# Mask added on VectorE in the maximum of the logits, and three rearrangements: first loads, banks of the spatial gate, last token blocks

## The chip, the core and the metric

One core of a Trainium2 chip runs the whole program. Its engines work side by side, each through its own queue in order: TensorE (matrix products into PSUM, weights loaded ahead of each), VectorE and ScalarE (elementwise work, reductions along a row, evacuation of PSUM), GpSimd (here a few powers and masks), and SyncE, whose queue issues most of the DMAs. [...] The metric is the time of one execution in microseconds; less is better.

## The reference

Two layers on 512 tokens of width 1024, fp32, with a memory of 256 rows. Layer 0 mixes by a gated spatial unit over chunks of 128 tokens (6 groups) and by attention to the memory (4 heads of 64); layer 1 by causal attention with a forget gate (12 heads of 64) and again by memory attention. Both are followed by an output projection, a feed-forward of width 2816, and norms. The parts that the change touches:

```python
def block(args):                      # forgetting_attention, one block of 128 queries
    i, qi, ci = args
    qpos = i * Q_BLOCK + jnp.arange(Q_BLOCK)
    logits = jnp.einsum('bthd,bshd->bhts', qi, k).astype(jnp.float32) * scale
    logits = logits + ci[..., :, None] - cT[..., None, :]
    mask = kpos[None, :] <= qpos[:, None]
    logits = jnp.where(mask, logits, -jnp.inf)
    p = jax.nn.softmax(logits, axis=-1).astype(v.dtype)
    return jnp.einsum('bhts,bshd->bthd', p, v)
...
s = jnp.einsum('gts,bcsgd->bctgd', w, vc) + b_s.T[None, None, :, :, None]   # spatial gating
...
f = (jax.nn.silu(f @ w_ffn_gate[layer]) * (f @ w_ffn_up[layer])) @ w_ffn_down[layer]
h = h + rmsnorm(f, ln_ffn_post[layer])                                      # the end of a layer
```

## The kernel before

**Arithmetic and layout.** Activations lie transposed: features on the 128 partitions, 512 tokens along the row, eight tiles for 1024 features. Each fp32 product is three products of rounded parts (`mm3`, L191: hi x hi, hi x lo, lo x hi), accumulated in one PSUM bank. Every weight is loaded as fp32 into one of four `raw` buffers and split into hi (ScalarE, cast) and lo (VectorE, subtract) by `split` (L240). PSUM banks come from three rings: `mm` and `lg` with three banks each, `tr` with two. A tile's bank is free again when its last reader is done, and within a bank the program keeps reads and writes of the same tile apart.

**Order.** A planner puts the instructions of each engine into a queue: by their place in the program, and by when its own costs let them start. `tc.issue_after` (and `behind`, L249) holds an instruction behind another in that order, and `high_priority` moves it forward. On the chip each queue then runs in order and waits by semaphore.

**Start.** `layer_a` (L566) loads the query weights (`query_weights`, two matrices of 512 KB, here half of the first, all of the second, the rest of the first) and the input x (`tokens`, eight tiles of 256 KB, cut in two parts each by `normed_parts`) on SyncE's queue. Sixteen products of three passes (L646) alternate between two outputs, tile by tile, with two dummy products of zeros (`idle`) after the first product of each output. Value and gate products of the gated unit follow as filling between later steps.

**Spatial gate.** `gate_inputs(m)` (L699) makes one block of the gate (24 passes, ring mm). `rows` (L761) are two tiles in ring lg that VectorE folds into the bias `bsp` (L768). `spatial(g)` (L728) makes two PSUM tiles `s`, both in ring lg, each read by ScalarE and VectorE.

**Attention.** `FoxHead.logits(tb)` (L499) makes the logits of 128 queries against the (tb+1) x 128 keys that they may see: one product of the head's parts (L504), one with the rest of the parts and the gate's sums (L505), and one in bf16 that adds the constant `neg` (0 on and below the diagonal, -1e30 above) to the last 128 columns, as identity times `neg` (L506). `weigh` (L437) takes the negated maximum of the row from the bank (VectorE, L440), then exp with that as bias and the row sum as second output (ScalarE, L441) into an SBUF tile p. `norm` divides (L450), `turn` transposes p (TensorE, L457) and splits it, `values` (L517) multiplies with the values. `attend` (L531) staggers this: while one head's logits are made, the head before is transposed and multiplied, and pieces of other work (`between`: key and value products, later the output projection) are laid between in a fixed count per head, five in the first heads, three in the last. There are 12 heads with four blocks of queries each, so 48 mask products.

**End.** `tail_of` (L785) makes, for each block tb of 128 tokens, the last share of the down projection into two banks of 512 columns (ring mm and lg); for the last block the second is cut in two halves of 256 columns (L806), both in the same bank. VectorE adds the earlier share (L816), ScalarE squares and sums (L819), VectorE adds up (L821), GpSimd takes the power (`rsqrt`, r), and ScalarE, in the last block VectorE too, scales by r. `give` (L1359) then transposes the block back (L847), adds it with the gain as per-partition scalar to h, one 128 x 128 piece at a time (`residual`, L852), and sends it out. `give(tb - 1)` stands behind `tail(tb)`; after the last, eight dummy products and `give` of block 3.

Of the kernel before, what the change touches and what calls it, by code (L numbers as in the profile page):

```python
# [7 lines left out]
F32 = mybir.dt.float32  # L8
# [32 lines left out]
def hybrid(ctx: ExitStack, tc: tile.TileContext, i: dict, out: bass.AP):  # L41
# [6 lines left out]
    sp = ctx.enter_context(tc.tile_pool(name="small", bufs=8))  # L48
    pp = ctx.enter_context(tc.tile_pool(name="psum", bufs=3, space=PSUM))
# [69 lines left out]
    G.affine_select(out=neg_f[:, :P], in_=neg_f[:, :P], pattern=[[-1, P]], compare_op=ALU.is_ge,  # L119
                    fill=NEG, base=0, channel_multiplier=1)  # L120
    neg = cp.tile([P, P], BF16, name="neg")
    V.tensor_copy(neg, neg_f[:, :P])
# [307 lines left out]
    class Softmax:  # L430
# [6 lines left out]
        def weigh(self, tb, lg, p):  # L437

            c = slice(tb, tb + 1)
            V.reduce_max(out=self.nmx[:, c], in_=lg, axis=AX.X, negate=True)  # L440
            last_exp[0] = A.activation(p, lg, AF.Exp, bias=self.nmx[:, c], accum_out=self.sm[:, c])  # L441
            self.p[tb] = p
# [47 lines left out]
    class FoxHead(Softmax):  # L490
# [8 lines left out]
        def logits(self, tb):  # L499
            qa, qc, ka, kc = self.parts  # L500
            n = (tb + 1) * P
            c = slice(tb * P, n)
            lg = ps("lg", s="lg")
            PE.matmul(lg[:, :n], qa[:, c], ka[:, :n], start=True, stop=False)  # L504
            PE.matmul(lg[:, :n], qc[:68, c], kc[:68, :n], start=False, stop=False)  # L505
            PE.matmul(lg[:, c], ident_b, neg, start=False, stop=True)  # L506
# [58 lines left out]

    def layer_a():  # L566
# [18 lines left out]
        tokens(0, 1)  # L585
        query_weights(1, 0, 1024)
        tokens(1, 2)
        tokens(2, 4)
# [3 lines left out]
        last_a = tuple(last_parts)  # L592
        vg, evacs = {}, []
# [28 lines left out]
        with tc.tile_pool(name="sgu", bufs=1) as lp:  # L622
# [105 lines left out]
            def spatial(g):  # L728
                t = temp("s", (P, TB, P))
                for tp2 in range(2):  # L730
                    o = ps("lg", (P, 2, 2, P), s="s")
                    hi, lo = vp[g // 2, tp2]
                    c = slice((g % 2) * P, (g % 2 + 1) * P)
                    for n in range(2):
                        PE.matmul(o[:, n, :, :], hi[:, n, c], ws[g], start=True, stop=True)
                        PE.matmul(o[:, n, 0, :], lo[:, n, c], ws[g][:, 0, :], start=False, stop=True, skip_group_check=True)
                    two = t[:, 2 * tp2 : 2 * tp2 + 2, :]
                    A.activation(two, o[:, :, 1, :], AF.Copy, scale=vcols[:, g : g + 1])
                    V.scalar_tensor_tensor(out=two, in0=o[:, :, 0, :], scalar=vcols[:, g : g + 1], in1=two,
                                           op0=ALU.mult, op1=ALU.add)  # L740
# [17 lines left out]
            V.tensor_copy(vcols, o)  # L758

# [25 lines left out]
    def tail_of(xs, load, ys, eps=None, last=False):  # L785
# [12 lines left out]
        def tail(tb, halfway=None):  # L798
# [4 lines left out]
            c = slice(tb, tb + 1)  # L803
            final = last and tb == TB - 1
            two = small("two", 1) if final else None
            at = [(0, 0, 4), (1, 0, 2), (1, 2, 4)] if final else [(0, 0, 4), (1, 0, 4)]  # L806
            for n, (dh, m0, m1) in enumerate(at):
                if m0 == 0:
                    o = ps("lg" if dh else "mm", s="y")
                cols = slice(m0 * P, m1 * P)  # L810
                for k in range(nk):
                    w = [part[:, m0:m1, :] for part in ws[k // 2, dh][k % 2]]
                    end = token_products(o[:, cols], xs[k], w, tb, k == 0, k == nk - 1)
                y = ys[tb][dh][:, cols]
                with urgent(tb):
                    V.tensor_add(y, o[:, cols], y)  # L816
# [3 lines left out]
                    if n == len(at) - 1:  # L820
                        V.scalar_tensor_tensor(out=v[:, c], in0=one, scalar=run, in1=eps[:, c] if eps is not None else rms_eps,  # L821
# [10 lines left out]
            if final:  # L832
                for m in (0, 2):
                    cols = slice(m * P, (m + 2) * P)
                    V.tensor_scalar_mul(ys[tb][1][:, cols], ys[tb][1][:, cols], r[:, c])
                    A.activation(ys[tb][0][:, cols], ys[tb][0][:, cols], AF.Copy, scale=r[:, c])
                return end
            with urgent(tb):
                for y in ys[tb]:
                    A.activation(y, y, AF.Copy, scale=r[:, c])  # L840

        return tail, ys

    def turned(ys, k, tbs, out):

        for n, tb in enumerate(tbs):
            PE.transpose(out[:, n * P : (n + 1) * P], ys[tb][k // 4][:, k % 4 * P : (k % 4 + 1) * P], ident)  # L847
# [510 lines left out]

    def give(tb, order, queues=(nc.sync,)):  # L1359
# [79 lines left out]
```

## Time and profile before

| | |
|---|---|
| median of 3 runs | 1113.27 us (1113.27 to 1113.5) |
| the profiled execution, its time | 1111.68 us |
| its span, first to last instruction | 1110.0 us |
| mean granted TensorE clock | 0.999 |
| opening: first product of the queries to the last one's start | 5.56 to 19.02 us |
| stage of the 12 masked heads | 613 to 718 us |
| from the last product's start to the span's end | 1101.05 to 1110.0 us |

The times of instructions are from the profiled execution. Busy time counts an engine as busy while any of its instructions runs; products on TensorE are pipelined, so their durations overlap, and the chain of work (each step followed back to what released it) tells better how long each one holds the queue. The mean of a group is of one instruction from start to end. In rows of windows stand: the stretch, its length, then busy time and count for TensorE, its weight loads, VectorE, ScalarE and GpSimd, the granted clock, the share of DMA and GB/s. In rows of a timeline: start, length, engine, line, operation, output and inputs, and in brackets the idle time before it and what ended it.

### The profile page before, as it was taken

The numbers are of one execution on the slowest core, as the hardware profiler recorded it, in microseconds if no ns is written. First come the engines' busy times: TensorE is split into PE (matmuls) and PEld (weight loads), VectorE is DVE, ScalarE is ACT, GpSimd is POOL, SyncE is SP. The second block draws the span as 40 slices with busy tenths as digits, with TensorE's granted clock in tenths as the row PEclk, the third lists the DMA queues.
The fourth block names the chain that finished last, engine by engine and source line by source line (L and its number), as shares of the span: only waits on it lengthen the run. The fifth ranks groups of instructions, "written<-read, shape, count | busy, mean of one in ns | idle before, by whom it ended". The sixth has DMA issues, their size and how long they took to land.

```text
span 1110.0 us, 19527 instructions
## 1 busy us (share of the span) xinstructions
PE 1100.9 (99%) x7384; PEld 999.7 (90%) x7385; DVE 895.0 (81%) x1734; ACT 667.1 (60%) x1401; POOL 25.1 (2%) x41
## 2 busy tenths in 40 slices
PE   9999999999999999999999999999999999999998
PEld 6997889999899899998988897889999899899996
DVE  7879659897698598787868889868897698588775
ACT  7776578664366254477647667768665266254453
POOL 0000000000000000001000000000000000000000
PEclk9999999999999999999999999999999999999999
DMA  7521331334135133245222555431234134233222
GB/s 268 159 79 58 113 116 39 115 115 136 55 115 152 56 96 115 79 150 173 77 76 75 155 124 131 129 115 39 77 97 151 58 115 134 58 114 114 77 76 77
DMA packets 63558, 118.13 MB, mean 106 GB/s; under 512 B 5164, under 2 KB 39992, under 8 KB 63464
## 3 DMA queue, kind: packets, MB, share of 16 engines
q1 hardware_dynamic: 62584, 116.05, 34.4%
q8 instruction: 58, 0.95, 0.4%
q0 software_dynamic: 192, 0.52, 0.2%
q10 hardware_dynamic: 688, 0.31, 0.1%
q14 instruction: 36, 0.29, 0.1%
HBM read 104.71 MB, written 2.10 MB: 96 GB/s over the span
## 4 chain that ended last, share of the span: by engine, by line
PE 86%; DVE 3%; ACT 1%; issue 1%; DMA 0%; POOLq 0%; POOL 0%; DVEq 0%; ACTq 0%
PE y L193 10%; PE y L194 10%; PE y L195 10%; PE a L194 5%; PE a L195 5%; PE a L193 5%; PE ps L193 3%; PE ps L194 3%; PE ps L195 3%; PE x L194 3%; PE x L195 3%; PE x L193 3%; PE e L193 3%; PE e L194 3%; PE e L195 3%; PE tr L457 1%
## 5 line engine op out<-in xcount | busy, mean ns | idle before, releaser
L241 ACT CAST whi<-raw 128x512 fp32r<-128x512 f32 x460 | 277.2, 620 | 266.6 <-PE y L195 118.5
L241 DVE TENSOR_TENSOR wlo<-raw,whi 128x512 fp32r<-128x512 f32 x460 | 306.3, 686 | 117.0 <-ACT whi L241 114.6
L193 PE MATMUL y<-whi,fhi 128*128 128x512 f32 (+1 forms) x356 | 139.7, 393 | 0.0
L194 PE MATMUL y<-wlo,fhi 128*128 128x512 f32 (+1 forms) x356 | 139.5, 392 | 0.0
L195 PE MATMUL y<-whi,flo 128*128 128x512 f32 (+1 forms) x356 | 139.1, 391 | 0.0
L194 PE MATMUL x<-xslo,whi 128*128 128x256 f32 x320 | 89.9, 281 | 0.0
L194 PE MATMUL a<-xslo,whi 128*128 128x256 f32 x320 | 89.9, 281 | 0.0
L195 PE MATMUL x<-xshi,wlo 128*128 128x256 f32 x320 | 89.8, 280 | 0.0
L193 PE MATMUL x<-xshi,whi 128*128 128x256 f32 x320 | 89.7, 280 | 0.0
L195 PE MATMUL a<-xshi,wlo 128*128 128x256 f32 x320 | 89.7, 281 | 0.0
L193 PE MATMUL a<-xshi,whi 128*128 128x256 f32 x320 | 89.6, 280 | 0.0
L195 PEld LDWEIGHTS y<-whi,flo 128*128 128x128 f32 x356 | 66.9, 188 | 15.5 <-DVE flo L241 0.2
L193 PEld LDWEIGHTS y<-whi,fhi 128*128 128x128 f32 x356 | 66.9, 188 | 15.1 <-DVE y L816 0.2
L194 PEld LDWEIGHTS y<-wlo,fhi 128*128 128x128 f32 x356 | 66.9, 188 | 14.7 <-DVE wlo L241 0.2
L193 PE MATMUL ps<-xshi,whi 128*128 128x256 f32 (+1 forms) x224 | 68.4, 306 | 0.0
L194 PE MATMUL ps<-xslo,whi 128*128 128x256 f32 (+1 forms) x224 | 66.7, 298 | 0.0
L195 PE MATMUL ps<-xshi,wlo 128*128 128x256 f32 (+1 forms) x224 | 66.4, 298 | 0.0
L193 PEld LDWEIGHTS a<-xshi,whi 128*128 128x128 f32 x320 | 60.3, 189 | 0.4
L194 PEld LDWEIGHTS a<-xslo,whi 128*128 128x128 f32 x320 | 60.2, 188 | 0.3
L193 PEld LDWEIGHTS x<-xshi,whi 128*128 128x128 f32 x320 | 60.3, 188 | 0.0
L195 PEld LDWEIGHTS x<-xshi,wlo 128*128 128x128 f32 x320 | 60.2, 188 | 0.0
L194 PEld LDWEIGHTS x<-xslo,whi 128*128 128x128 f32 x320 | 60.2, 188 | 0.0
(289 smaller groups left out, 3082.1 us busy)
## 6 DMA issues: line engine op xcount, KB each, us to landing
raw<-in_w_gate SPq DMA_DIRECT2D x44, 512.0 KB
raw<-in_w_up SPq DMA_DIRECT2D x44, 512.0 KB
raw<-in_w_down SPq DMA_DIRECT2D x44, 512.0 KB
raw<-in_w_out SPq DMA_DIRECT2D x16, 512.0 KB
raw<-in_w_b_q SPq DMA_DIRECT2D x8, 512.0 KB
raw<-in_w_a_v SPq DMA_DIRECT2D x6, 512.0 KB
raw<-in_w_a_u SPq DMA_DIRECT2D x6, 512.0 KB
raw<-in_w_v SPq DMA_DIRECT2D x6, 512.0 KB
```

Source lines behind the costliest of these rows:

```text
L193: PE.matmul(o, w[0], x[0], start=start, stop=False, skip_group_check=more)
L194: PE.matmul(o, w[0], x[1], start=False, stop=False, skip_group_check=more)
L195: return PE.matmul(o, w[1], x[0], start=False, stop=stop, skip_group_check=more)
L241: last_parts[:] = A.copy(hi, src), (eng or V).tensor_sub(lo, src, hi)
L457: PE.transpose(tr[:, at * P : (at + 1) * P], src, ident)
```

## The change

- **Mask.** The mask product L506 goes, and with it the bf16 identity. `neg` becomes 512 columns wide (zeros, then the triangle in the last 128), so that its last n columns mask a block of n keys. `weigh` gets the mask: one VectorE instruction adds it to the logits, multiplies by -1, writes the result to p in SBUF and takes the minimum of the row; exp then reads p with scale -1 and writes over it. Memory heads keep the plain maximum.
- **First loads.** x tiles 0 to 3 come one by one ahead of the second query matrix, which is loaded in halves, its second half last of all. The products take four tiles for output 0, then the same four for output 1, then the other four. The dummy products between them go.
- **Spatial gate.** The first of the two tiles `s` takes ring mm, the second lg.
- **End.** The gain of the last norm is turned into a row (one transpose, a copy, a write to DRAM in the spatial stage) and spread over all partitions by a DMA behind block 0. In blocks 2 and 3 y is multiplied by it ahead of the scale by r, in the second half of block 3 together with it. The two halves of block 3 have banks of their own. `give_added` transposes and adds groups of two or four pieces at once. Block 2's transposes stand behind the last product of block 3, its third add behind the last sum; six dummy products remain.

```diff
@@ constants
-    ident_b = cp.tile([P, P], BF16, name="ident_b")
-    V.tensor_copy(ident_b, ident)
...
-    neg = cp.tile([P, P], BF16, name="neg")
-    V.tensor_copy(neg, neg_f[:, :P])
+    neg = cp.tile([P, T], BF16, name="neg")
+    V.tensor_copy(neg, neg_f)
@@ Softmax
-        def weigh(self, tb, lg, p):
+        def weigh(self, tb, lg, p, mask=None):
             c = slice(tb, tb + 1)
-            V.reduce_max(out=self.nmx[:, c], in_=lg, axis=AX.X, negate=True)
-            last_exp[0] = A.activation(p, lg, AF.Exp, bias=self.nmx[:, c], accum_out=self.sm[:, c])
+            if mask is None:
...
+            else:
+                V.tensor_tensor_reduce(out=p, in0=lg, in1=mask, scale=-1.0, scalar=-NEG, op0=ALU.add, op1=ALU.min,
+                                       accum_out=self.nmx[:, c])
+                last_exp[0] = A.activation(p, p, AF.Exp, bias=self.nmx[:, c], scale=-1.0, accum_out=self.sm[:, c])
@@ FoxHead.logits
-            PE.matmul(lg[:, :n], qc[:68, c], kc[:68, :n], start=False, stop=False)
-            PE.matmul(lg[:, c], ident_b, neg, start=False, stop=True)
+            PE.matmul(lg[:, :n], qc[:68, c], kc[:68, :n], start=False, stop=True)
...
-            self.weigh(tb, lg[:, :n], (self.beside if tb == 0 else self.room)[:, at : at + n])
+            self.weigh(tb, lg[:, :n], (self.beside if tb == 0 else self.room)[:, at : at + n], neg[:, T - n :])
@@ new
+    def row_of_gains(block):
+        gain_row[0] = dp.tile([KT, P], F32, name="row")
+        o, row = ps("tr", (KT, P), s="gr"), temp("row", (KT, P))
+        PE.transpose(o, gains[:, block * KT : block * KT + KT], ident)
+        A.copy(row, o)
+        nc.scalar.dma_start(gain_row[0], row)
+
+    def spread_gains():
+        row = gain_row[0]
+        gain_row[0] = wp.tile([P, D], F32, tag="raw", name=name("raw"), bufs=4)
+        nc.sync.dma_start(gain_row[0], row.rearrange("a b -> (a b)").partition_broadcast(P))
@@ layer_a
         query_weights(0, 0, 512)
-        tokens(0, 1)
-        query_weights(1, 0, 1024)
-        tokens(1, 2)
-        tokens(2, 4)
+        for k in range(4):
+            tokens(k, k + 1)
+        query_weights(1, 0, 512)
         query_weights(0, 512, 1024)
         tokens(4, 6)
         tokens(6, 8)
         last_a = tuple(last_parts)
+        query_weights(1, 512, 1024)
...
-            for k in range(KT):
+            for half in range(0, KT, 4):
                 for o, w in zip(outs, wq):
-                    end = mm3(o, w[k], a[k], k == 0, k == KT - 1)
-                    if k == 0:
-                        idle(2, zero, end)
+                    for k in range(half, half + 4):
+                        mm3(o, w[k], a[k], k == 0, k == KT - 1)
...
-                    o = ps("lg", (P, 2, 2, P), s="s")
+                    o = ps(("mm", "lg")[tp2], (P, 2, 2, P), s="s")
...
+            row_of_gains(G_FFN_POST + 1)
@@ tail_of
+            added = last and tb >= TB - 2
             final = last and tb == TB - 1
+            if added:
+                gained[tb] = [plain("yg") for _ in range(2)]
...
-                if m0 == 0:
-                    o = ps("lg" if dh else "mm", s="y")
-                cols = slice(m0 * P, m1 * P)
+                cols, own = slice(m0 * P, m1 * P), slice(0, (m1 - m0) * P)
+                o = ps("lg" if dh > m0 else "mm", s="y")
...
+                    if added and not (final and dh):
+                        V.tensor_mul(gained[tb][dh][:, cols], y, gain_row[0][:, 512 * dh + m0 * P : 512 * dh + m1 * P])
...
-                    V.tensor_scalar_mul(ys[tb][1][:, cols], ys[tb][1][:, cols], r[:, c])
-                    A.activation(ys[tb][0][:, cols], ys[tb][0][:, cols], AF.Copy, scale=r[:, c])
-                return end
+                    y0, y1 = (y[:, cols] for y in gained[tb])
+                    V.scalar_tensor_tensor(out=y1, in0=ys[tb][1][:, cols], scalar=r[:, c],
+                                           in1=gain_row[0][:, 512 + m * P : 512 + (m + 2) * P],
+                                           op0=ALU.mult, op1=ALU.mult)
+                    A.activation(y0, y0, AF.Copy, scale=r[:, c])
+                return end, total
@@ the end
+    def give_added(tb, order, tags, queues=(nc.sync,), end=None, held={}):
+        c = (tb * P, (tb + 1) * P)
+        for n, some in enumerate(order):
+            tr = ps(tags[n], (P, len(some), P), s="yt")
+            k0, k1 = some[0], some[-1] + 1
+            with behind([end] if end else ()):
+                for x, k in enumerate(some):
+                    row_turned(gained[tb], k, tr[:, x, :])
+            with behind(held.get(n, ())):
+                V.tensor_add(h[:, k0:k1, c[0] : c[1]], tr, h[:, k0:k1, c[0] : c[1]])
+            queues[n % len(queues)].dma_start(out[:, k0:k1, c[0] : c[1]], h[:, k0:k1, c[0] : c[1]])
...
     for tb in range(TB):
-        end = tail(tb)
-        if tb:
+        end, sums = tail(tb)
+        if tb == 0:
+            spread_gains()
+        elif tb < TB - 1:
             give(tb - 1, (range(4), range(4, 8)))
-    idle(8, zero, end)
-    give(TB - 1, (range(4, 6), range(2), range(6, 8), range(2, 4)), (nc.sync, nc.scalar))
+    give_added(TB - 2, (range(2), range(2, 4), range(4, 8)), ("tr", "tr", "mm"), end=end, held={2: [sums]})
+    idle(6, zero, end)
+    give_added(TB - 1, (range(4, 6), range(2), range(6, 8), range(2, 4)), ("lg", "mm") * 2, (nc.sync, nc.scalar))
```

More of the change, by code (lines that the diff above doesn't have):

```diff
@@ L48, in hybrid @@
     sp = ctx.enter_context(tc.tile_pool(name="small", bufs=8))
+    dp = ctx.enter_context(tc.tile_pool(name="rows", bufs=1, space=bass.MemoryType.DRAM))
     pp = ctx.enter_context(tc.tile_pool(name="psum", bufs=3, space=PSUM))
@@ L820, in tail @@
                     if n == len(at) - 1:
-                        V.scalar_tensor_tensor(out=v[:, c], in0=one, scalar=run, in1=eps[:, c] if eps is not None else rms_eps,
+                        total = V.scalar_tensor_tensor(out=v[:, c], in0=one, scalar=run, in1=eps[:, c] if eps is not None else rms_eps,
                                                op0=ALU.add, op1=ALU.add)
@@ L846, in turned, with row_turned @@
         for n, tb in enumerate(tbs):
-            PE.transpose(out[:, n * P : (n + 1) * P], ys[tb][k // 4][:, k % 4 * P : (k % 4 + 1) * P], ident)
+            row_turned(ys[tb], k, out[:, n * P : (n + 1) * P])
+    def row_turned(y, k, out):
+        PE.transpose(out, y[k // 4][:, k % 4 * P : (k % 4 + 1) * P], ident)
     def residual(o, k, cols, post):
```

12 lines of the change are left out of this document (8 added, 4 removed).

## The prediction

> **What bounds the kernel now.** I read the page first: span, busy time, and the chain of work that ended last.
>
> ```profile
> span 1110.0 us, 19527 instructions
> PE 1100.9 (99%) x7384; PEld 999.7 (90%) x7385; DVE 895.0 (81%) x1734; ACT 667.1 (60%) x1401; POOL 25.1 (2%) x41
> PE 86%; DVE 3%; ACT 1%; issue 1%; DMA 0%; POOLq 0%; POOL 0%; DVEq 0%; ACTq 0%
> ```
>
> TensorE is the bound nearly everywhere: 86% of the chain is its products. So an edit is worth what it takes out of TensorE's queue, a stall or an instruction, unless VectorE (81%) is late in that stage. TensorE's waits over the whole run are few. The two that the change can touch, beside the end of the kernel, are these:
>
> ```profile
> PE s L735 <- DVE bsp L768: 1.1, 1, 1.1
> PE ps L194 <- DVE alo L246: 0.6, 2, 0.3
> ```
>
> The first is one stall of 1.1 us in the spatial gate; the second belongs to the opening, where the first inputs arrive. So there are four places to price: attention, opening, spatial gate, end.
>
> **Attention: the mask.** Next, in that stage (613 to 718 us), the chain in order of time and the groups by line:
>
> ```profile
> 614.75 0.24 PE lg L505
> 614.99 0.07 PE lg L506
> 615.07 0.44 PE tr L457 x4
> ...
> 615.86 0.07 PE lg L506
> 615.93 0.17 PE v L193
> 616.11 0.12 PE v L194
> ...
> L506 PE MATMUL lg<-neg,ident_b 128*128 128x128 bf16 x48 | 11.1, 231 | 0.0
> L440 DVE TENSOR_REDUCE nmx<-lg 128x1 f32<-128x512 f32 (+3 forms) x48 | 22.9, 483 | 3.5 <-PE lg L506 3.2
> ```
>
> A group's 231 ns is latency; in the chain a mask product holds the queue for 0.07 us. Where an ordinary product follows, that one takes 0.17 instead of its usual 0.12 us, because its weights load less hidden; before transposes there is no such extra. One of four masks of a head is surely followed so, perhaps two. Gross: 48 x 0.07 = 3.4 us, plus 12 to 24 x 0.05 = 0.6 to 1.2 us; I take 4.3 us, 0.09 per mask.
>
> The cost lies on VectorE. 48 plain maxima (mean 483 ns) become 48 fused add-and-minimum instructions that read the logits, read the mask, write 128xN to SBUF and deliver one number per row. No such instruction is in this trace, so it is bounded by rows. Reading a second tensor and computing twice:
>
> ```profile
> L440 DVE TENSOR_REDUCE nmx<-lg 128x1 f32<-128x256 f32 x12 | 5.0, 418 | 1.0 <-PE lg L506 0.9
> L739 DVE SCALAR_TENSOR_TENSOR s<-s,vcols,s 128x256 f32<-128x256 f32 x2 | 0.9, 475 | 0.0
> L440 DVE TENSOR_REDUCE nmx<-lg 128x1 f32<-128x128 f32 x12 | 3.4, 283 | 0.2
> L852 DVE SCALAR_TENSOR_TENSOR h<-yt,gains,h 128x128 f32<-128x128 f32 x32 | 9.3, 343 | 0.1
> L441 ACT ACTIVATION_READ_ACCUMULATOR p<-lg,nmx 128x1 f32 x48 | 9.7, 202 | 0.0
> ```
>
> Two-tensor, two-operation reads of PSUM cost 0.06 us more than the maximum at both sizes. The lower end is 0: an instruction with one pass over N columns is not shorter than the maximum, which makes the same pass. The upper end is ScalarE's separate read-out of its sum, 0.20 us. I take +0.06 us, the rows of the same engine and operand places. The exp now reads p in SBUF and not the bank; ScalarE has room (67 and 77% busy in the stretches below), and the bank is freed earlier, by the maximum and not by the exp.
>
> Has VectorE the room? The stage in two stretches (length, then busy PE, PEld, DVE, ACT):
>
> ```profile
> 614.30:661.00 46.70, 46.70 (x328) 41.45 (x326) 40.98 (x96) 31.51 (x81) 0.00 (x0) 1.00 0.50 132
> 661.00:717.00 56.00, 55.41 (x328) 45.38 (x327) 52.53 (x124) 43.33 (x113) 0.00 (x0) 1.00 0.55 139
> ```
>
> In the first five heads VectorE idles 5.7 us of 46.7; 20 masks add 1.2 us, and TensorE's saving of 20 x 0.09 = 1.8 us fits in what is left. In the last seven it idles only 3.5 of 56 us, and TensorE itself already shows 0.6 us without work. If half of that idle time can be used (my choice; the rest is spent waiting for results), 28 masks cost 28 x 0.06 = 1.7 us against 1.7 us of room: no gain. **Attention: -1.8 us**, where the masks alone are worth -4.3. With +0 per instruction it is -1.8 - 1.7 = -3.5; with +0.20 it is about -1.7 + (5.6 - 1.7) = +2.2.
>
> [...]
>
> **The opening.** Loads now come as: half of weights 0, x tiles 0 to 3 one by one, half of weights 1, second half of 0, x 4-5, x 6-7, second half of 1. The products run four of output 0, four of output 1, and so on, and the four pairs of dummy products go.
>
> ```profile
> 3.86 0.62 ACT L241 CAST whi<-raw 128x512 fp32r<-128x512 f32 x1 [1.11 <-DMA raw<-in_w_a_q]
> 4.79 0.72 ACT L245 ACTIVATE ahi<-h,gains 128x512 fp32r<-128x512 f32 x1 [0.31 <-DMA h<-in_x]
> 9.29 1.34 ACT L245 ACTIVATE ahi<-h,gains 128x512 fp32r<-128x512 f32 x2 [0.55 <-DMA h<-in_x]
> 5.56 0.50 PE L193 MATMUL ps<-ahi,whi 128*128 128x512 f32 x1 [0.34 <-ACT ahi L245]
> 19.02 0.40 PE L195 MATMUL ps<-ahi,wlo 128*128 128x512 f32 x1
> 4.79:10.16 5.37, 4.46 (x16) 1.87 (x14) 3.60 (x8) 3.45 (x6) 0.00 (x0) 1.00 0.96 342
> 10.16:19.25 9.09, 9.09 (x40) 7.32 (x39) 8.80 (x14) 9.01 (x17) 0.00 (x0) 1.00 1.03 406
> ```
>
> From 10.16 us on, 39 products fill 9.09 us, 0.233 each; all 48 need 11.2 us but take from 5.56 to 19.25 = 13.7. So 2.5 us are lost, all before 10.16. Arrivals: between 3.86 and 9.29 us 1.5 MB came behind the first, 0.9 us per 256 KB. So x 1, 2, 3 arrive near 5.7, 6.7, 7.6 us. Each needs ScalarE (0.72) and VectorE (about as long) and gives 0.7 us of products: the first twelve end near 9.6. Weights 1 land at 8.5 and are split by 9.9, so the next twelve run gapless to 12.4. By then x 4-5 (near 11) are cut, x 6-7 (12.5) cost some 0.5 us of waits, and the last half of weights (13.2) is split by about 15: the end lies near 18.1. **Opening: -1.1 us**, between 0 (later x tiles as late as now) and -1.5. What follows, the value products, finds its weights: nothing waits there now, and the bytes ahead of them are the same. The wider mask constant costs one longer cast on VectorE, hidden in its waits before 10 us.
>
> **The spatial gate.** s takes its first bank from the ring mm, the second from lg.
>
> ```profile
> 96.98 0.22 PE L736 MATMUL s<-ws,vlo 128*128 128x128 f32 x1
> 98.33 0.36 PE L735 MATMUL s<-ws,vhi 128*128 128x256 f32 x1 [1.13 <-DVE bsp L768]
> 100.00:110.00 10.00, 10.00 (x48) 8.25 (x47) 10.00 (x21) 5.56 (x11) 0.00 (x0) 1.00 0.25 76
> ```
>
> Two rows tiles and the first s hold all three lg banks, so the second s waits until VectorE has read rows. With mm that wait goes. Late next could be VectorE, full from 100 to 110 us: the 1.1 us come back only where TensorE then overtakes it. The nearest case, the split weights of the fifth gate block, is over a microsecond early by the order of the rows, so I take **-1.1 us**, from -1.3 to -0.2. The new transpose of gains costs TensorE 0.11 us (615.07: four in 0.44); its copy and DMA issue on ScalarE lie where that engine idles 44%: **+0.1 us**.
>
> **The end.** The last half of token block 3's products gets a bank of its own; block 2's transposes move behind the last product; gains are multiplied in beforehand, so that plain adds of 256 or 512 columns replace eight 128-column ones.
>
> ```profile
> 1098.83 0.28 PE L195 MATMUL y<-whi,flo 128*128 128x256 f32 x1
> 1099.63 0.39 PE L193 MATMUL y<-whi,fhi 128*128 128x256 f32 x1
> 1101.05 0.28 PE L195 MATMUL y<-whi,flo 128*128 128x256 f32 x1
> 1102.67 0.54 POOL L262 TENSOR_TENSOR r<-v,mhalf 128x1 f32<-128x1 f32 x1 [6.28 <-DVE v L821]
> 1103.24 0.61 DVE L835 TENSOR_SCALAR y<-y,r 128x256 f32<-128x256 f32 x2 [0.40 <-POOL r L262]
> 1103.77 2.75 DVE L852 SCALAR_TENSOR_TENSOR h<-yt,gains,h 128x128 f32<-128x128 f32 x9
> L816 DVE TENSOR_TENSOR y<-y,y 128x256 f32<-128x256 f32 x2 | 0.8, 424 | 1.3 <-PE y L195 1.3
> L816 DVE TENSOR_TENSOR y<-y,y 128x512 f32<-128x512 f32 x6 | 4.1, 690 | 5.9 <-PE y L195 5.9
> ```
>
> Products with 256 columns start 0.12 us apart, so the first half is through at 1098.95, and the second could start then and not at 1099.63: -0.7. Behind r VectorE now works 0.6 + 8 x 0.31 = 3.1 us; afterwards two scaled multiplies (at most 0.9, by L739) and four adds of 256 columns (4 x 0.37 without their overlap): 2.4. So -0.7 more. Block 2's third add is held behind the sum and takes 0.6 us beside POOL's 0.54; the three added multiplies (0.69 each) lie in the 5.9 us in which VectorE waits for products. The 512 KB broadcast of gains waits on SP's queue for a raw buffer that the last weights give back when they are split; it goes out behind the first block, two blocks (some 11 us) ahead of its use, and only block 0's output is queued behind it. Block 2's transposes now wait for the last product; the dummy products and block 3's transposes are queued behind them, and those wait for r anyway. SP issues one transfer more, in that same pause. **End: -1.4 us**, from -0.5 (a late third add, or transposes that crowd the last ones) to -2.0.
>
> **The sum.** -1.8 - 1.1 - 1.1 + 0.1 - 1.4 = -5.3 us. The profiled execution took 1111.68 us (span 1110.0 plus 1.7 around it): 1106.4. The median before is 1113.27, 1.6 above that execution; on that scale **1108.0 us**.
>
> **Rivals.** A, **the ends only**: opening and gate give their 2.2 us back, because VectorE is full from 100 to 110 us and the planner, which orders the queues by its own costs, may place work differently. For it: those full rows; against it: TensorE waits nowhere between the opening and 97 us. Time: 1113.27 - 1.8 - 1.4 + 0.1 = 1110.2, still faster. B, **VectorE becomes the bound of attention** with 0.20 us per fused instruction: +2.2 - 3.5 = -1.3, 1112.0, no change. C, the other side: **the fused instruction runs at half rate**. The four sizes have 320 columns on average, and 128 columns cost 418 - 283 = 0.135 us, so it costs +0.34. The first heads then add 6.8 - 5.7 = +1.1, the last 9.5 - 1.7 = +7.8; with -3.5 elsewhere +5.4: 1118.7. It decides from about +0.28 us per instruction on (48 x 0.28 - 7.4 = +6.0 in attention against -3.5 elsewhere). For it: a read of two tensors and a write in one instruction is nowhere in the trace together with a reduction; against it: two-tensor reads here run at the rate of one.
>
> **How the numbers follow.** Forecast 0.62, A 0.18, B 0.12, C 0.08. A measurement of this kernel can tell about 0.2%, 2.2 us: faster is under 1111.0, slower over 1115.5. Faster: forecast and A, 0.80; same: B, 0.12; slower: C, 0.08. The range takes the low ends together (-4.3 - 1.5 - 1.3 - 2.0, near -9) and reaches over B to just above the old time: 1104.2 to 1113.5. C lies outside, with some of the tails.
>
> **What would show it.** Fused instructions of 0.34 to 0.75 us, 0.06 above today's maxima: right; a second row behind each: B. TensorE's last opening product near 18 us; no wait of s on bsp; the last two halves of block 3 0.12 us apart; VectorE's last add 2.4 us behind r. In the last seven heads VectorE above 95% busy. The forecast is wrong if heads get longer, if the fused instruction passes 0.28 us extra, or if TensorE shows new waits between 20 and 150 us.

## The result, and the profile after

The changed kernel takes 1107.31 us in the median (1106.43 to 1108.74) against 1113.13 (1111.94 to 1113.5) for the kernel before beside it: a ratio of 0.9950, interval 0.9937 to 0.9963. That is 5.8 us less; 5.3 were forecast. The total hides misses in both directions, so the parts count. The page of the profiled execution (1106.43 us):

```profile
span 1104.7 us, 19453 instructions
PE 1096.6 (99%) x7332; PEld 999.0 (90%) x7332; DVE 896.1 (81%) x1775; ACT 667.5 (60%) x1402; POOL 24.8 (2%) x41
PE 94%; DVE 2%; ACT 1%; DMA 1%; issue 1%; SPq 0%; POOLq 0%; POOL 0%; DVEq 0%; ACTq 0%
```

TensorE has 52 recorded products fewer, 48 of them the masks, and is still the bound. What it waits for now, without the wait of the first dummy product at the start and one of 0.2 us at the end (in us: in all, times, longest):

```profile
PE ps L191 <- ACT ahi L243: 0.6, 1, 0.6
PE tr L460 <- DVE p L453: 0.4, 2, 0.2
PE ps L192 <- DVE alo L244: 0.3, 1, 0.3
PE lg L507 <- DMA ka<-whi: 0.3, 1, 0.3
```

The 1.1 us of the second s on bsp is gone; new is a product of the late heads that waits for a DMA.

To compare kernels I cut each trace at the start of the same products: opening (to the first value product), gate (first s to the next gate product), the first five masked heads, the last seven (to the last product with values), and the end (from the transposes of block 1 to the span's end). The end has three pieces: until r is there, until the last add, until the span's end. In us, one profiled execution each (the sixth head's start, which parts five from seven, is read to a tenth of a us, so seven is good to 0.05):

```
kernel              opening  gate  five   seven  end    = r    + adds + out   span
before               19.25   2.24  46.3   65.14  16.10   9.34   3.32   3.43   1110.0
changed              18.82   0.92  44.5   64.48  15.01   8.64   2.49   3.88   1104.7
e1 mask alone        20.50   2.66  44.5   65.38  16.13   9.37   3.32   3.44   1110.5
e2 all but the mask  19.07   0.92  46.3   65.26  14.97   8.62   2.49   3.86   1107.0
e3 no mask           18.92   0.92  44.5   63.75  16.86   8.65   2.49   5.73   1105.8
e4 mask twice        18.33   0.92  46.3   65.84  14.99   8.63   2.49   3.88   1107.0
e5 hold x2           22.11   0.92  44.5   64.24  15.13   8.60   2.48   4.04   1108.0
e6 banks only        19.58   2.24  46.3   65.09  18.70   8.57   6.69   3.44   1112.7
e7 values, GpSimd    19.01   0.92  44.5   63.29  14.66   8.64   2.49   3.53   1104.5
e8 more on GpSimd    19.92   0.92  44.9   65.26  14.67   8.64   2.49   3.55   1108.3
e9 hold, in order    20.88   0.92  44.5   64.91  15.16   8.63   2.49   4.04   1108.8
e10 late values      18.93   0.92  44.5   63.34  15.60   8.63   2.49   4.47   1104.4
e11 late copies      19.32   0.92  44.5   63.69  14.42   8.64   2.49   3.30   1104.1
e12 e10 and e11      20.16   0.92  44.5   64.71  14.44   8.65   2.49   3.30   1105.8
```

From before to changed: opening -0.4, gate -1.3, first heads -1.8, last heads -0.7, end -1.1. Between these stand +0.25 behind the opening, +0.47 between the gate and the first head and -0.7 between the last head and the end, which cancel. The +0.47 comes as differences of some 5 ns over hundreds of products, in e2 as in the changed kernel and not in e1 or e6, so it belongs to the rearrangements; the cause stays open.

Three of these executions lost time to the clock: the granted clock was 0.50 for 3.41 us from 99.46 us in e1, from 1104.24 in e6 and from 7.91 in e12. So e1's gate, e6's adds and e12's opening are longer than their edits made them.

**The fused instruction.** VectorE's groups in the attention stage of the changed kernel (busy, mean ns of one, idle before):

```profile
L442 DVE CUSTOM_DVE_ANT_0 p<-lg,neg 128x512 f32<-128x512 f32 x12 | 8.2, 685 | 1.5 <-PE lg L508 1.5
L442 DVE CUSTOM_DVE_ANT_0 p<-lg,neg 128x384 f32<-128x384 f32 x12 | 6.6, 548 | 0.0
L442 DVE CUSTOM_DVE_ANT_0 p<-lg,neg 128x256 f32<-128x256 f32 x12 | 5.1, 421 | 0.8 <-PE lg L508 0.7
L442 DVE CUSTOM_DVE_ANT_0 p<-lg,neg 128x128 f32<-128x128 f32 x12 | 3.3, 278 | 0.0
L442 DVE DVE_READ_ACCUMULATOR2_ANT nmx<- 128x1 f32 x48 | 4.0, 84 | 0.0
```

The main part takes what the plain maximum took (418 ns at 256 columns, 283 at 128): the 0.06 us that the forecast added are not there. A second row of 84 ns reads the accumulator out. Does it cost 84 ns of VectorE? VectorE's timeline of the changed kernel, and below it the one of before:

```profile
658.93 0.68 DVE L442 CUSTOM_DVE_ANT_0 p<-lg,neg 128x512 f32<-128x512 f32 x1
659.54 0.08 DVE L442 DVE_READ_ACCUMULATOR2_ANT nmx<- 128x1 f32 x1
659.54 0.69 DVE L239 TENSOR_TENSOR mixedlo<-f,mixedhi 128x512 fp32r<-128x512 f32 x1
```

```profile
663.44 0.68 DVE L440 TENSOR_REDUCE nmx<-lg 128x1 f32<-128x512 f32 x1
664.04 0.68 DVE L241 TENSOR_TENSOR pT<-tr,pT 128x512 fp32r<-128x512 f32 x1
```

The read and the next instruction start at the same time, 0.61 us behind the main part; behind a plain maximum the next starts after 0.60. At 384, 256 and 128 columns the medians are 0.47, 0.35 and 0.21 us against 0.47, 0.34 and 0.20, so they differ by 0.01 at most. So the mask costs VectorE about 0.01 us, not 0.084. The windows over all of the last seven heads agree: VectorE is busy 56.02 us before and 56.05 after.

```profile
660.60:725.74 65.14, 64.55 (x377) 52.99 (x374) 56.02 (x132) 47.02 (x119) 0.00 (x0) 1.00 0.49 125
```

```profile
657.80:722.28 64.48, 63.52 (x348) 52.25 (x346) 56.05 (x160) 47.47 (x120) 0.00 (x0) 1.00 0.49 127
```

The trace has two rows for each fused instruction, and the second starts together with its successor (both at 659.54 us above). So a second row behind each fused instruction, which the forecast had named as the sign of rival B, did appear and was no sign of B's cost.

### The profile page after: what moved, and what is told of

Its sections match the earlier page's. It is cut to its first block, busy times and chain, and to the rows that moved or that the text cites. A ratio compares the mean times of both kernels' runs of the same rounds, so it can differ in the third digit from the quotient of the medians.

```text
span 1104.7 us, 19453 instructions
## 1 busy us (share of the span) xinstructions
PE 1096.6 (99%) x7332; PEld 999.0 (90%) x7332; DVE 896.1 (81%) x1775; ACT 667.5 (60%) x1402; POOL 24.8 (2%) x41
## 4 chain that ended last, share of the span: by engine, by line
PE 94%; DVE 2%; ACT 1%; DMA 1%; issue 1%; SPq 0%; POOLq 0%; POOL 0%; DVEq 0%; ACTq 0%
PE y L191 10%; PE y L193 10%; PE y L192 10%; PE a L191 5%; PE a L193 5%; PE a L192 5%; PE ps L191 4%; PE ps L193 4%; PE ps L192 4%; PE e L193 3%; PE e L191 3%; PE x L193 3%; PE x L191 3%; PE e L192 3%; PE x L192 3%; PE v L191 2%
```

## Experiments

### The parts one by one: e1, e2, e3, e4

e1 is the kernel before with the mask's lines of the diff alone; e2 has all other lines and keeps the mask on TensorE.

> Only the mask is changed (fused instruction on VectorE, no mask product); loads, banks and end are those of before. Stage lengths of before and of the changed kernel: first five heads 46.3 and 44.6 us, last seven heads up to the last values product 65.1 and 64.5. Theory 1 (the stage stands by itself): the same gain here, -1.7 and -0.6, and the whole kernel 2 to 3 us faster than before (ratio 0.9975 to 0.998). Theory 2 (part of the stage's gain came from earlier starts of the other parts, so that transfers for the heads arrive in time): the last seven heads gain nothing or lose here, and the whole is under 1.7 us faster.

> The mask product and the plain maximum stay; loads, banks and end are those of the changed kernel. Theory 1: heads as before (46.3 and 65.1 us), opening -0.4 (first value product near 18.8 instead of 19.25 us), spatial stall gone (from the first s product to the next gate product 0.9 instead of 2.2 us), end -1.1; the whole 3 us faster than before (ratio near 0.997). Theory 2 (parts hang together): the sum of this run's gain and of the run with the mask alone differs from the whole change's 5.8 us by over 1.5 us.

Measured: e1 1109.95 us, ratio 0.9976 (0.9967 to 0.9986); e2 1109.37, 0.9973 (0.9963 to 0.9983). By these ratios they gain 2.7 and 3.0 us on that chip (1111.98 before), which add up to the whole change; each interval reaches about 1.1 us to either side, so only a mutual effect of more than some 1.5 us is excluded. e1's first heads gain 1.8 us as theory 1 has it. Its last seven lose 0.2, as theory 2 has it: a product there waits 1.1 us for the copy of keys (below, under e11).

e3 leaves the causal mask out on both engines, e4 does the masking on both:

```diff
@@ e3
-            self.weigh(tb, lg[:, :n], (self.beside if tb == 0 else self.room)[:, at : at + n], neg[:, T - n :])
+            self.weigh(tb, lg[:, :n], (self.beside if tb == 0 else self.room)[:, at : at + n], None)
@@ e4
...
-            PE.matmul(lg[:, :n], qc[:68, c], kc[:68, :n], start=False, stop=True)
+            PE.matmul(lg[:, :n], qc[:68, c], kc[:68, :n], start=False, stop=False)
+            PE.matmul(lg[:, c], ident_b, neg[:, T - P :], start=False, stop=True)
```

> The changed kernel with the causal mask left out on both engines: plain maximum, no mask product, exp reads the bank. So TensorE's saving is there in full and VectorE has 48 accumulator reads of 0.084 us (4.0 us) less than in the changed kernel. Theory 1 (VectorE holds the last seven heads): first five heads stay at 44.6 us, last seven fall from 64.5 to 62.5 to 63.2 us, near the gross saving of 28 x 0.09. Theory 2 (VectorE does not hold them, the order of copies and other transfers on SyncE's queue does): last seven heads stay at 64 to 65 us. Theory 3 (a mask product was worth less than 0.09 us of TensorE): first five heads stay, last seven fall by less than 0.5.

> The changed kernel with the mask product kept as well, so the mask is added twice. TensorE has before's work, VectorE the changed kernel's. Theory 1: first five heads back to 46.3 us or a little over (VectorE has room there), last seven over 65.1: 66 to 67.5 us. Theory 2 (accumulator reads cost the stage nothing): 46.3 and 65.1 us, as before.

Measured: e3 1106.59 us (0.9936 to 0.9966), e4 1109.05 (0.9962 to 0.9982). The first five heads, 44.5 and 46.3, follow TensorE's masks alone. The last seven, 63.75 and 65.84, fall between the theories. I first read them as VectorE's work for the accumulator, and wrote so into later expectations; that reading fell with the timeline above. Where the difference lies stands under e11.

### The opening: e5, e9

The forecast had x1 to x3 come one behind the other. ScalarE's timeline of the changed kernel:

```profile
3.79 0.62 ACT L239 CAST whi<-raw 128x512 fp32r<-128x512 f32 x1 [1.04 <-DMA raw<-in_w_a_q]
4.53 0.72 ACT L243 ACTIVATE ahi<-h,gains 128x512 fp32r<-128x512 f32 x1
6.92 2.02 ACT L243 ACTIVATE ahi<-h,gains 128x512 fp32r<-128x512 f32 x3 [1.67 <-DMA h<-in_x]
8.90 1.29 ACT L239 CAST whi<-raw 128x512 fp32r<-128x512 f32 x2
```

x1 is late, and x2 and x3 lie ready behind it. To tell sharing from slowness, x2 was held until w0 is cast:

```diff
         for k in range(4):
+            if k == 2:
+                G.tensor_copy(h[:, 2, 0:1], wq[0][0][0][:, 0:1].bitcast(F32))
             tokens(k, k + 1)
```

> The changed kernel, with the third tile of x held back until the first half of w0 has been cast (about 4.5 us), so that only that half, x0 and x1 are in flight before; everything behind x2 on SyncE's queue moves back with it. Forecast's step: x1 would land at 5.7 us behind x0; in the changed kernel's profile ScalarE took x1, x2 and x3 up together at 6.92. Theory 1 (the transfers that are in flight share the 16 DMA engines, so that early tiles land late, and together): x1 is taken up at 4.9 to 5.6, x2 and x3 at 7 or later, and the opening ends later than 18.8, by the hold. Theory 2 (the transfers go in order, and are slow until about 6 us whatever is queued): x1 is still taken up at 6.2 or later.

e5 missed its aim: the planner put x3 and all other loads ahead of the held x2, so the queue stayed as full as before; x1 was taken up at 5.92, between the two theories, and x2 only at 12.53 (one execution, 1109.92 us). e9 keeps every later load behind x2:

> The hold of the earlier run once more, now with every later load kept behind x2 on SyncE's queue: until about 4.5 us only the first half of w0, x0 and x1 are in flight. Theory 1 (the transfers in flight share the DMA engines): x1 is taken up at 4.9 to 5.6, and x2 lands at 7 or later; the opening ends at 19.5 to 21. Theory 2 (the tiles come at the pace that the engines have in these first microseconds whatever is queued): x1 at 5.8 or later, as with seven tiles in flight (6.25 to 6.92, and 5.92 in the first hold).

```profile
4.17 0.62 ACT L239 CAST whi<-raw 128x512 fp32r<-128x512 f32 x1 [1.43 <-DMA raw<-in_w_a_q]
4.77 1.34 ACT L243 ACTIVATE ahi<-h,gains 128x512 fp32r<-128x512 f32 x2
8.52 1.33 ACT L243 ACTIVATE ahi<-h,gains 128x512 fp32r<-128x512 f32 x2 [2.42 <-DMA h<-in_x]
```

With three transfers in flight x1 is there when ScalarE is done with x0 (5.40 us), as theory 1 has it (one execution, 1110.79 us). With seven in flight it was taken up between 5.43 and 7.01 in the nine profiles with the new order, 6.41 in the middle. The bytes tell the theories apart. In e9, x1 is taken up when 768 KB have gone over SyncE's queue, which is just the half of w0, x0 and x1; they were over at 4.98 us. In the nine the first 768 KB were over at 4.7 to 5.3 us too, but in seven of them ScalarE stood waiting for x1 until 1010 to 1310 KB had gone. So parts of later tiles went ahead of the last part of x1: the tiles do not come one behind the other. Whether the transfers take turns, or some of the 16 DMA engines lag, the traces do not tell. For the tiles behind x1 a second reason is in the rate. The windows from 4 to 6 us, changed kernel and before:

```profile
4.00:6.00 2.00, 2.00 (x5) 0.59 (x3) 1.41 (x2) 1.13 (x2) 0.00 (x0) 1.00 0.84 246
```

```profile
4.00:6.00 2.00, 1.66 (x5) 0.43 (x3) 1.15 (x2) 1.20 (x2) 0.00 (x0) 1.00 0.95 339
```

93 GB/s less for 2 us are 186 KB, some 0.6 us of arrivals. In each of the nine unheld profiles with the new order the rate falls under 240 GB/s between 4.6 and 5.2 us, in none of the three with the old one (286 to 420 there). The old order has such dips at other times (e1 154 GB/s near 3.9 us, e6 205 from 5.4 to 6.0), and what makes the rate fall was not tried.

### The end: e6

e6 is the kernel before with a bank of its own for each part of the last products:

```diff
-                if m0 == 0:
-                    o = ps("lg" if dh else "mm", s="y")
-                cols = slice(m0 * P, m1 * P)
+                cols, own = slice(m0 * P, m1 * P), slice(0, (m1 - m0) * P)
+                o = ps("lg" if dh > m0 else "mm", s="y")
...
```

> The kernel before, with a bank of its own for each part of the last block's products and nothing else of the change. Theory 1 (the forecast's step: the addition of the second part no longer holds back the products of the third): from the last block's first row product to r 8.6 us instead of 9.34, the adds behind r still 3.32, the rest of the end 3.4; all else as before, 1109.3 us in the profiled span. Theory 2 (the 0.70 came with the multiplication by the row of gains or with the other order of block 2's results): 9.2 to 9.4.

Block 2's transposes in the kernel before, between the last two parts, and in e6, behind the last product, with what follows there:

```profile
1098.95 0.71 PE L847 MATMUL yt<-ident,y 128*128 128x128 f32 x5
```

```profile
1100.55 1.04 PE L846 MATMUL yt<-ident,y 128*128 128x128 f32 x8
1103.55 2.93 PE L88 MATMUL idle<-zeros 128*128 128x512 bf16 x7 [1.97 <-DVE h L851]
1106.28 1.06 PE L846 MATMUL yt<-ident,y 128*128 128x128 f32 x4
1106.95 2.33 DVE L851 SCALAR_TENSOR_TENSOR h<-yt,gains,h 128x128 f32<-128x128 f32 x8 [2.42 <-PE yt L846]
```

r comes after 8.57 us instead of 9.34: theory 1. But the adds miss their number by far, 6.69 instead of 3.32, and the one execution took 1114.44 us. Before, five of block 2's transposes filled the time in which the third part could not start; now all eight come behind the last product, and VectorE's adds of block 2 come later with them. The dummy products wait 1.97 us for these adds, which must free a bank of ring tr; behind this wait the granted clock is 0.50 for 3.41 us, and the dummy products start 0.43 us apart instead of 0.22. Block 3's transposes are queued behind them, and VectorE stands idle 2.42 us for the first. So in this order of the queues the banks' 0.7 us are lost again. The rest of the edit puts block 3's transposes into the rings lg and mm and empties tr by plain adds of two or four pieces.

### The last seven heads: e7, e8, e10, e11, e12

e7 gives the low parts of the heads' values to GpSimd, e8 those of queries, keys and mixed rows too:

```diff
@@ e7, e8
-                    split(src.rearrange("p a (b c) -> p a b c", b=2), dst[:, :, :, 0, :], dst[:, :, :, 1, :])
+                    split(src.rearrange("p a (b c) -> p a b c", b=2), dst[:, :, :, 0, :], dst[:, :, :, 1, :], G)
@@ e8
-            split(qs[pr], *pair["q"])
-            split(keys[pr], *pair["k"])
+            split(qs[pr], *pair["q"], G)
+            split(keys[pr], *pair["k"], G)
...
-            return lambda: split(joined[m], *mixed[m])
+            return lambda: split(joined[m], *mixed[m], G)
```

> The changed kernel, with the low parts of the heads' values (in the last seven heads 5 subtractions of 0.42 us, 2.1 us of VectorE) computed on GpSimd. Theory 1 (VectorE's load sets a part of the last seven heads, at 0.28 us of the stage for each us of VectorE's work, as the reads of the accumulator cost 0.65 to 0.73 for 2.35): last seven heads 63.9 instead of 64.48, 0.6 us less in all. Theory 2 (it was the latency between the logits and the exponential alone that cost; load elsewhere is covered): 64.4 to 64.6, no change.

> As the run with the values' low parts on GpSimd, and there too the low parts of queries and keys (4 subtractions of 0.68 us in the last seven heads) and of the mixed rows (4 of 0.69): 7.5 us of VectorE's 52.8 in that stage go to GpSimd. Theory 1 (load): last seven heads 62.4 to 62.9, 2 us less. Theory 2 (latency, and transfers in SyncE's order): 64.3 to 64.6, or more where GpSimd's slower subtraction of queries and keys makes the copies to the other partitions late: then the wait for ka grows.

e7: 1106.54 us (0.9937 to 0.9967); the last seven fall to 63.29, more than expected, but 0.94 us come up ahead of the first head. e8: 1108.83 (0.9959 to 0.9982) and 65.26, a miss: nothing waits for ka there, and TensorE waits 1.8 us for p. Its GpSimd groups show why a subtraction there is no gift: VectorE takes 0.68 us for 512 columns.

```profile
L239 POOL TENSOR_TENSOR mixedlo<-f,mixedhi 128x512 fp32r<-128x512 f32 x7 | 9.9, 1417 | 25.8 <-ACT mixedhi L239 25.8
L239 POOL TENSOR_TENSOR wlo<-q,whi 128x512 fp32r<-128x512 f32 x6 | 8.1, 1354 | 32.1 <-ACT whi L239 32.1
```

e10 keeps e7's edit for the last six heads alone; e11 moves their copies of queries and keys to GpSimd's queue:

```diff
@@ e10
+                    split(src.rearrange("p a (b c) -> p a b c", b=2), dst[:, :, :, 0, :], dst[:, :, :, 1, :], G if u.pr >= 3 else None)
@@ e11
-                nc.sync.dma_start(dst.bitcast(F32), src[own, :].bitcast(F32))
+                (nc.gpsimd if u.pr >= 3 else nc.sync).dma_start(dst.bitcast(F32), src[own, :].bitcast(F32))
```

> The changed kernel, with the low parts of the values of the last six heads alone on GpSimd (6 subtractions of 0.42 us off VectorE; GpSimd took 0.83 us for each in the run that moved all twelve). There the last seven heads fell to 63.29 and 0.94 us came up ahead of the first head. Theory 1 (VectorE's load sets part of the last seven heads; the 0.94 came with the early heads' values, which now stay): last seven heads 63.3 to 63.7, x0 to the first head 409.9, 1105.9 to 1106.5 us in the median of the kernel whose changed form gave 1107.3, and a ratio of 0.9935 to 0.9945 to before. Theory 2 (the 1.19 was a chance of the order in which the planner then set the queues): 64.2 to 64.6.

> The changed kernel, with the copies of queries and keys between partitions (six of 128 KB per head) of the last six heads given by GpSimd's queue instead of SyncE's, where they stand among the loads of w_out. Theory 1 (VectorE's load and latency hold the last seven heads): 64.2 to 64.8. Theory 3 (the copies come late behind w_out's loads in SyncE's order; the product waited 0.7 us for ka in the changed kernel and 1.1 with the mask alone): the wait for ka goes, last seven heads 63.3 to 63.8.

e10: 1105.26 us, ratio 0.9935 (0.9922 to 0.9949), last seven 63.34: theory 1's numbers for the stage and the ratio, with a median 0.6 us under its range. It is the best kernel here by its median, though its interval overlaps the changed kernel's. e11: 63.69 (one execution, 1105.8 us): theory 3's number. The weight loads' waits for ka (in all, times, longest) in the changed kernel, e5 and e9, whose attention is the same:

```profile
PEld lg L507 <- DMA ka<-whi: 0.7, 1, 0.7
```

```profile
PEld lg L507 <- DMA ka<-whi: 0.4, 1, 0.4
```

```profile
PEld lg L510 <- DMA ka<-whi: 0.9, 1, 0.9
```

e3, e10 and e11 have no such wait. It comes ahead of the tenth head's logits. To see what it costs I cut the stage at each head's first product of logits (us):

```
                ninth to tenth   eleventh to twelfth   the other five
before               6.85               8.68               49.62
e2 all but mask      6.84               8.70               49.67
e4 mask twice        6.96               9.09               49.80
changed              6.89               9.04               48.59
e1 mask alone        7.77               9.06               48.53
e5 hold x2           6.58               9.05               48.58
e9 hold, in order    7.04               9.04               48.86
e11 late copies      6.50               8.67               48.50
e3 no mask           6.30               8.26               49.17
e10 late values      6.08               8.05               49.19
```

Five of the seven stretches gain 0.8 to 1.1 us together whatever the loads and copies do (changed, e1, e5, e9, e11 against before). The other two gain nothing. From the ninth head to the tenth the time goes with the wait for ka, from 6.50 without it (e11) to 7.77 (e1). From the eleventh to the twelfth no wait for ka is on record. There the mask on VectorE itself costs 0.4 us: e4 against e2, which have the same products on TensorE. e11 takes this 0.4 us away and e10 1.0; whether the late copies or VectorE's order holds TensorE in that stretch is not shown.

So what kept the last seven heads above 63.7 is in part the copy of keys that comes behind a load of w_out on SyncE's queue, as e11 shows. SyncE's queue in the changed kernel:

```profile
682.09 0.37 SPq L167 DMA_DIRECT2D raw<-in_w_out  x1
682.51 0.52 SPq L1340 DMA_DIRECT2D qa<-whi  x1
683.07 2.54 SPq L1340 DMA_DIRECT2D qa<-wlo  x1
685.66 1.23 SPq L1340 DMA_DIRECT2D ka<-whi  x2
```

In the chain the first copy behind the load, one of queries, stands so:

```profile
682.51 5.59 DMA qa<-whi
```

5.59 us for a copy that takes 2.3 in the median of that stage (DMA issues: KB each, us to landing):

```profile
qa<-whi SPq DMA_DIRECT2D x6, 128.0 KB, 2.3
```

The copies of keys are issued 3.2 us behind it, and the product that needs them starts at 689.27 us. VectorE's load is the likeliest reason for e10's lead of 0.4 us over e3 and e11 (54.49 instead of 56.1 us busy), but the planner sets other queues anew as well, so this is not isolated.

e12 makes both edits.

> The changed kernel with both edits for the last six heads: the low parts of the values on GpSimd (last seven heads 63.34 alone) and the copies of queries and keys by GpSimd's queue (63.69 alone), against 64.48. If the two take away separate waits, their gains of 1.14 and 0.79 add up: 62.4 to 62.8, and some 1104.5 to 1105 us. If they loosen the same place (VectorE and the transfers in turn ahead of the same products), or if GpSimd's 0.83 us of subtraction now stand ahead of the copies in its own queue: 63.2 to 63.6, and the time of the values' edit alone, 1105.0 to 1105.8.

e12: 1107.40 us (0.9942 to 0.9969), last seven 64.71, outside both expectations: the gains do not add up, and the stage is longer than with either edit. VectorE and GpSimd in e12:

```profile
689.10 1.58 DVE L453 TENSOR_SCALAR p<-p,sm 128x512 f32<-128x512 f32 x2
691.27 0.81 DVE L453 TENSOR_SCALAR p<-p,sm 128x256 f32<-128x256 f32 x1
```

```profile
689.71 0.75 POOL L239 TENSOR_TENSOR vals<-vf,vals 128x256 fp32r<-128x256 f32 x1
690.80 1.14 POOL L239 TENSOR_TENSOR vals<-vf,vals 128x256 fp32r<-128x256 f32 x1 [0.34 <-ACT vals L239]
```

```profile
L453 DVE TENSOR_SCALAR p<-p,sm 128x256 f32<-128x256 f32 x8 | 2.8, 351 | 0.1
```

The last row is the changed kernel's: 0.35 us for what took 0.81 while GpSimd subtracted, and TensorE's transposes waited 2.1 us for p. In e10, with the same subtractions on GpSimd and the copies on SyncE, no such scaling takes over 0.52 us. In e12 the first subtraction starts (689.71 us) where GpSimd's issue of a copy ends (689.69), so the copies seem to have moved it beside the scalings. What lengthened the scalings is not shown: the order of the starts is too rough in the trace to tell who held whom.

## Why the prediction was right, point by point

- **First five heads**, -1.8 forecast, -1.8 measured: right, for the reason given (TensorE's masks of 0.09 us, VectorE with room; e3 and e4 confirm it).
- **The fused instruction**, +0.06 us: the mis-sized term. It holds VectorE for 0.01 us more, close to the lower bound of 0; rivals B and C, which needed 0.20 and 0.34, fall. New is a dearer exp, below.
- **Last seven heads**, 0 forecast, -0.66 measured: the step that put 1.7 us of new work on VectorE failed, for its busy time did not change (56.02 and 56.05 us). With an instruction that costs 0 the forecast's own figure is -1.7; e11, where no copy is late, gives -1.45, and in the changed kernel copies and VectorE's order in two of the heads take 0.8 back. That VectorE has little room there was not wrong: without any mask (e3) the stage gains 1.4 of the 2.5 us that TensorE gives up, and with 1.6 us less on VectorE (e10) 1.8. The forecast had no term for the copies on SyncE's queue.
- **Opening**, -1.1 forecast, -0.4 in the pair of profiles, -0.6 by the middle of nine new (19.01) against three old (19.58): the step "x 1, 2, 3 arrive near 5.7, 6.7, 7.6 us" failed. Taken up in the middle case at 6.4 and 7.7, x1 and x2 are 0.7 and 1.0 us late, because later tiles take part of the bytes. Old and new openings scatter by 1.3 and 1.8 us, more than the gain. The longest new one, e12's 20.16, is the one with the clock at 0.50. The dummy products that go are two pairs (four products), not the four pairs of the forecast.
- **Spatial gate**, -1.1 forecast, -1.32 measured, the upper end: no wait is left between the two s, and in the 140 us behind it no product is more than 0.15 us later, counted from the gate's end. So rival A falls: e2, the rearrangements without the mask, is 2.6 to 3.0 us faster, where A left them 1.3.

```profile
96.86 0.33 PE L752 MATMUL s<-ws,vhi 128*128 128x256 f32 x1
97.25 0.22 PE L753 MATMUL s<-ws,vlo 128*128 128x128 f32 x1
97.31 0.45 PE L191 MATMUL ps<-ahi,whi 128*128 128x512 f32 x1
```

- **End**, -1.4 forecast, -1.1 measured. -0.70 before r as forecast, and e6 shows that the banks alone give it, with block 2's transposes moved behind. The adds gave 0.83 instead of 0.7. What failed is a term left out: from the last add to the end it now takes 0.45 us more. The DMA's rates (40 slices of the last 7.7 us changed, 8.0 us before):

```profile
GB/s 0 0 0 0 0 27 287 258 194 301 250 61 277 290 287 293 197 3 0 37 255 309 277 266 306 290 287 282 290 125 0 0 0 0 0 0 0 0 0 0
```

```profile
GB/s 289 289 292 131 0 0 0 0 0 0 0 0 0 0 0 169 297 274 307 284 259 307 289 259 297 289 225 151 302 215 8 0 0 0 0 0 0 0 0 41
```

Before, one train of 768 KB, block 2's second half and then block 3, went out in 3.0 us and ended 1.5 us behind the last add. Now block 2 is out of the way, block 3's 512 KB go in 2.0 us at about the same rate, and they end 1.9 us behind the last add. The adds end 0.8 us sooner and the transfers only 0.4. The 1.9 us stand in nine of the eleven profiles with this end; in e3 and e10 the transfers were slower (3.8 and 2.8 us). From the last packet to the span's end 1.4 to 2.1 us pass, so a few tenths of this piece are chance.

That the total came so close is luck in part: the opening and the end fell short by 1.0 us, and the late heads and the gate brought 0.9 more.

## What to carry to other kernels

A fused instruction is priced by the distance from its start to the next one's (here 0.61 us at 512 columns), not by adding up the rows it leaves (0.685 and 0.084). Where a stage does not respond to an engine's load, look for transfers that stand behind large loads on the same queue (here one of 5.59 us, with a median of 2.3), and compare kernels head by head, so that one such wait does not hide the rest. An order that fits with one edit (banks, idle products, copies) can turn bad with half of it, as in e6 (adds of 6.69 us instead of 3.32), or with another beside it, as in e12 (64.71 us for the last seven heads, 63.34 and 63.69 with either edit alone).

## What the runs showed of the hardware

In the changed kernel exp over 512 columns, from SBUF and with scale -1, took 0.035 us longer than before from PSUM with scale 1 (727 against 692 ns in the mean); the groups of the changed kernel and of before:

```profile
L444 ACT ACTIVATE p<-p,nmx 128x512 f32<-128x512 f32 x12 | 8.7, 727 | 2.5 <-DVE nmx L442 2.5
```

```profile
L441 ACT ACTIVATE p<-lg,nmx 128x512 f32<-128x512 f32 x12 | 8.3, 692 | 3.0 <-DVE nmx L440 3.0
```

A subtraction of two tensors took GpSimd twice VectorE's time (in e8 1.35 us in the mean for the queries, in e10 0.68 on VectorE, both at 512 columns). In e12 a scaling of 256 columns by VectorE took 0.81 us while GpSimd subtracted; in the changed kernel the eight of that form took 0.35 in the mean.

The granted clock fell to 0.50 for 3.41 us in e1, e6 and e12: in e1 and e6 during or behind waits of TensorE (1.1 and 1.97 us), in e12 in the opening. In e5's opening TensorE waited 2.16 us for x2 and the mean clock of that execution was 1.0, so what makes it fall can't be read from these runs.
